# Sums of merged blocks formed behind the merges and kept in DRAM, one plain output pair in place of two, and three planner costs

## The chip, the core and the metric

The kernel runs on one core of a Trainium2 chip. The metric is the device time of one execution in microseconds; three runs of the kernel before the change took 1144.78, 1145.87 and 1147.69 us, median 1145.87.

## What is computed

One encoder layer is applied to two batches with the same weights: a prompt of 512 tokens and a sample of 1024, 1024 channels wide, all in float32.

```python
h = rmsnorm(x, norm_g)
qa, ka, va, za, qb, kb, vb, zb, ga, gb = split(h @ w_in)
oa = (neighbourhood_attention(rms(qa), rms(ka), va, rpb) * silu(za)) @ w_o_a
ob = (window_gqa_attention(rms(qb), rms(kb), vb, t5, sink) * silu(zb)) @ w_o_b
merged = sigmoid(ga) * oa + sigmoid(gb) * ob
y = x + merged @ w_out
```

The last line is the one on which most of the change bears: for the sample, merged is 1024 x 1024 and w_out is 1024 x 1024.

## The kernel before, in words

Every operand of a matmul is held as a high part (rounded to fp32r) and a low part (the rest), and a product is made of three matmuls: high x high, high x low, low x high (`product`, L1276). The step that makes the two parts is `split` (L1163): ACT copies the high part, then DVE or POOL subtracts it from the source to give the low part. In the names, `hh` and `hl` are the parts of the normed input, and later of the merged values, which take its place; `whi` and `wlo` are those of a weight; `T` holds both parts of a moving operand that was made by sums or loaded; `U`, `C`, `S`, `ot` and `raw` are tiles of 128 x 512 in pools of 4, 5, 3, 2 and 4 buffers; `p`, `x` and `d` are the 2, 5 and 1 PSUM banks.

The stages follow each other: the prompt's attention, the prompt's dense phase, the sample's attention, the sample's dense phase (`dense_phase`, L1136). In a dense phase the output projections are done in pairs of 128-channel chunks, in one of two ways. A plain pair (`pair_classic`, L1308) takes two chunks x two halves of the tokens x eight blocks of channels x three matmuls of 512 columns. A pair by Strassen's scheme (`pair_strassen`, L1320) takes seven products of four blocks x three matmuls: product 0 on the merged block (0,0), 1 on (1,0), 2, 3, 4 and 5 on the sums T1, T2, T0 and T3, and 6 on (1,1). It needs four sums of weights per pair (tiles `S`), and, once for all pairs, the four sums of merged blocks, each in four pieces k (`sums`, L1185): T0 = (0,1) - (0,0), T2 = (1,1) - (0,1), T1 = (1,1) - T0, T3 = T1 - (1,0). A piece takes 10 steps on DVE or POOL, since the high and low parts are added up one after the other, and then four splits into `T`. The eight `T` buffers hold the branch outputs until the last merge has read them.

A merge m (L1543) makes chunk m of the merged values: two products per half, gate values loaded back from `g_d` into `C` and `U`, two multiplications, one addition, one split into hh and hl. Merges run from m = 0 to 7 at priorities 12 to 19, the four output pairs at 20 to 23. `CLASSIC_S` = (1, 0, 2) says how many pairs of the sample are plain: one of the z projections, none of the gates, two of the output.

The order of all instructions on all five queues is made ahead of time by a list scheduler (`Flow`, L141): each operation has a list of engines with a cost in ns, a priority (lower first), the tiles it makes and reads, and what it must follow. When an engine is free in the planner's clock, it takes the ready operation of the lowest priority number for which buffers are free. DVE and POOL don't run steps with two SBUF operands at the same time in this plan. The attention's costs of ACT, DVE and POOL are multiplied by `SLACK` = 1.1. The plan fixes the order alone; on the chip each engine runs its own queue in order and waits for semaphores. All DMAs are issued by SP, in order. So a changed cost changes the order, here of both attention phases, and no work.

In the attention (`attention_phase`, L648) the steps named in the change are: the low parts of k and of q (DVE, L887 and L901, in `make_qk`), the strided copies `hb` of hh and hl that branch B reads (ACT L662 or DVE L664, in `project`), and the copies that turn rows into bias tables (ACT L662, in `tables`).

Of the kernel before, what the change touches and what calls it, by code (L numbers as in the profile page):

```python
# [10 lines left out]
F32 = mybir.dt.float32  # L11
# [16 lines left out]
SCRATCH = 1024  # L28
CLASSIC_P = (4, 8, 4)
SIDE = {5: 0, 8: 1, 11: 2, 15: 3}  # L30
CLASSIC_S = (1, 0, 2)
LEFT_PAD = 56
WAKE = 0
SOON = 10
# [106 lines left out]
class Flow:  # L141
# [46 lines left out]
    def dma(self, emit, nbytes, prio, **kw):  # L188
        return self.op((("sp", 470),), lambda e: emit(), prio, lag=nbytes / 360, **kw)
# [165 lines left out]
def encoder_kernel(  # L355
# [292 lines left out]
    def attention_phase(geo, hh, hl, h_ops, mask_d, early, late):  # L648
# [24 lines left out]
        def tables(br, g, prio):  # L673
            nb_t = tile_([P, max(2 * at[-1], 4 * GW)], F32, "bias", 2)
            first = [nb_t]
            for i in range(2 if br == "A" else 4):
                raw = tile_([P, max(GW, 48 * geo.cw)], F32, "raw", RAW[nt])
                if br == "A":
                    run, cw = 3 * geo.cw * 16, geo.cw
                    h = 2 * g + i  # L680
                    sp(
                        lambda raw=raw, h=h: nc.sync.dma_start(raw.t[:, :run], rpb_x[nt][h]),
                        run * 512, prio, new=[raw], after=expanded[nt, h],
                    )
                    for o, n, c0 in [(a + o, n, c0) for a, (_, runs) in zip(at, a_tables) for o, n, c0 in runs]:
                        nw = n // P * cw
                        for l in range(2):

                            def emit(e, i=i, o=o, n=n, c0=c0, nw=nw, l=l, raw=raw):
                                rv = raw.t[:, :run][:, ::-1].rearrange("p (c h l) -> p c l h", l=2, h=8)  # L690
                                rv = rv[:, c0 : c0 + nw, l, : geo.rh]
                                ov = nb_t.t[:, i * at[-1] + o : i * at[-1] + o + n]
                                ov = ov.rearrange("p (c l h) -> p c l h", l=2, h=geo.rh)[:, :, l]
                                mv = mask.t[:, o : o + n].rearrange("p (c l h) -> p c l h", l=2, h=geo.rh)[:, :, l]
                                engines[e].tensor_tensor(ov, mv, rv, op=ALU.subtract)

                            f.op(
                                (("dve", DVE_(n // 2)), ("pool", POOL_(n // 2))), emit, prio,
                                new=first, use=[raw, mask], into=[nb_t],
                            )  # L700
                            first = []
                else:
                    h = 4 * g + i

                    def emit_load(raw, h, lo):
                        ld = line_d[h : h + 1, :]
                        src = bass.AP(tensor=ld.tensor, offset=ld.offset + lo * 64, ap=[[1, 64], [1, GW]])
                        nc.sync.dma_start(raw.t[:, :GW].rearrange("(c l) f -> l c f", l=2)[lo], src)

                    for lo in range(2):  # L710
                        kw = {"new": [raw], "after": line_op} if lo == 0 else {"into": [raw]}
                        sp(lambda raw=raw, h=h, lo=lo: emit_load(raw, h, lo), 98304, prio, **kw)

                    def emit(e, i=i, raw=raw):
                        ov = nb_t.t[:, i * GW : (i + 1) * GW].rearrange("p (w c l) -> p w c l", w=3, l=2)
                        rv = raw.t[:, :GW][:, ::-1].rearrange("p (w l c) -> p w c l", w=3, l=2)
                        copy(e, ov, rv)

                    f.op((("act", ACT_(GW)),), emit, prio, new=first, use=[raw], into=[nb_t])
                    first = []  # L720
            return nb_t

# [5 lines left out]
        def project(br, w, t, prio):  # L728
# [5 lines left out]
            if br == "A":  # L734
                hs = h_ops[t]
                part = [lambda k, v=v: v.t[:, k, t * P : (t + 1) * P] for v in (hh, hl)]
                held = [[hh] * KC, [hl] * KC]
                done = {}
            else:

                hs = []
                hb = [[tile_([P, KC // 2, P], F32R, "hb", HB) for _ in range(2)] for _ in range(2)]
                part = [lambda k, v=v: v[k // 4].t[:, k % 4] for v in hb]
                held = [[v[k // 4] for k in range(KC)] for v in hb]
                done = {}
                for q in range(2):
                    for m, v in enumerate((hh, hl)):
                        done[m, q] = f.op(
                            (("act", 960), ("dve", DVE_(512))),
                            lambda e, m=m, v=v, q=q: copy(  # L750
                                e, hb[m][q].t, v.t[:, 4 * q : 4 * q + 4, t:nt:nb].bitcast(F32)
                            ),
                            prio - 1, new=[hb[m][q]], hold=[v], after=[o for u in h_ops.values() for o in u], port=True,
                        )
# [92 lines left out]
        def make_qk(br, gi, t, qk, prio):  # L847
# [23 lines left out]
            elif whole:  # L871
# [11 lines left out]
                prio, use=[pt, gains_v], after=old, **kw,  # L883
            )
            b = f.op(
                (("dve", DVE_(P) + 165),),
                lambda _: dve.scalar_tensor_tensor(  # L887
                    kt.t[:, k0 + 1, tok], pk(), gain_k[br], kt.t[:, k0, tok].bitcast(F32), op0=ALU.mult, op1=ALU.subtract
                ),
# [2 lines left out]
            for s in slots:  # L892
# [4 lines left out]
                prio, use=[pt, gains_v], into=[q],  # L897
            )
            f.op(
                (("dve", DVE_(n) + 165),),  # L900
                lambda _: dve.scalar_tensor_tensor(  # L901
                    qv(1), pts(), gain_q[br], qv(0).bitcast(F32), op0=ALU.mult, op1=ALU.subtract
                ),
# [232 lines left out]
    def dense_phase(geo, hh, hl, h_ops, o_stores, exps_done, start, opened, tp, up, p0, p1, p2, x_t, y_t, classic, fill, after_gates=None, side=None):  # L1136
# [7 lines left out]
        short = nt == nh  # L1144
        any_tt = lambda n: (("dve", DVE_(n)), ("pool", POOL_(n)))
        u_d = dpool.tile([8, P, nt], F32, tag=f"u_d{nt}", name=f"u_d{nt}")
        g_d = dpool.tile([2, 8, P, nt], F32, tag=f"g_d{nt}", name=f"g_d{nt}")
        stores = {}
        h_reads = []
# [32 lines left out]

            return mov

        def sums(prio, done):  # L1185

            tv = [tuple(f.value(tp, [P, 4, sn], F32R, "T", 8) for _ in range(2)) for _ in range(4)]
            ops = {}
            for k in range(4):
                blk = lambda a, kk, n: (lambda: a.t[:, kk, n * sn : (n + 1) * sn].bitcast(F32))  # L1190
                h = {(i, n, a): blk((hh, hl)[a], k + 4 * i, n) for i in range(2) for n in range(2) for a in range(2)}
                t = [tile_("S", 3) for _ in range(4)]

                def step(j, in0, block, part, op, new, other=None):
                    after = done[k + 4 * block[0], block[1]] if done else []
                    kw = {"new": [t[j]]} if new else {"into": [t[j]]}
                    use = [v for v in (other, None if new else t[j]) if v]
                    tt(
                        lambda v=t[j]: v.t[:, :sn], in0, h[*block, part], op, sn, prio, use=use, after=after, hold=[hh, hl], **kw
                    )  # L1200


                for j, plus, minus in ((0, (0, 1), (0, 0)), (2, (1, 1), (0, 1))):
                    after = done[k + 4 * plus[0], plus[1]] + done[k + 4 * minus[0], minus[1]] if done else []
                    tt(
                        lambda v=t[j]: v.t[:, :sn], h[*plus, 0], h[*minus, 0], ALU.subtract, sn, prio, new=[t[j]], after=after,
                        hold=[hh],
                    )
                    step(j, lambda v=t[j]: v.t[:, :sn], plus, 1, ALU.add, False)
                    step(j, lambda v=t[j]: v.t[:, :sn], minus, 1, ALU.subtract, False)  # L1210
                after = done[k + 4, 1] if done else []
                tt(
                    lambda v=t[1]: v.t[:, :sn], h[1, 1, 0], lambda v=t[0]: v.t[:, :sn], ALU.subtract, sn, prio,
                    new=[t[1]], use=[t[0]], after=after, hold=[hh],
                )
                step(1, lambda v=t[1]: v.t[:, :sn], (1, 1), 1, ALU.add, False)
                step(3, lambda v=t[1]: v.t[:, :sn], (1, 0), 0, ALU.subtract, True, t[1])
                step(3, lambda v=t[3]: v.t[:, :sn], (1, 0), 1, ALU.subtract, False)
                for j in (0, 2, 1, 3):
                    vh, vl = tv[j]  # L1220
                    ops[j, k] = split(
                        lambda vh=vh, k=k: vh.t[:, k], lambda vl=vl, k=k: vl.t[:, k], lambda v=t[j]: v.t[:, :sn], sn, prio,
                        (vh, k == 0), (vl, k == 0), [t[j]],
                    )

            return moving_sums(tv, ops)

# [352 lines left out]
                side(12 + m)  # L1580

        h_reads = []
        mov_h, mov_t = blocks(m_ops, nh), sums(20, m_ops) if o_classic < 4 else None
        for i in range(4):
            srcs = [[w_out[c, j] for j in range(2)] for c in (2 * i, 2 * i + 1)]
            post = lambda m, *a, i=i: post_out(2 * i + m, *a)
# [185 lines left out]
```

## Time and profile before

| | |
|---|---|
| median of three runs | 1145.87 us (1144.78 to 1147.69) |
| profiled execution, its own time | 1146.52 us |
| its span, first to last instruction | 1144.7 us |
| granted TensorE clock, mean | 1.000 |
| matmuls in the span | 6139 |

A record of a matmul lasts longer than the distance to the next one, since matmuls are pipelined; the distance between starts is what counts. The same holds, in a smaller measure, for steps of DVE and ACT. In lists of waits the columns are the total, the number of waits and the longest, in us.

### The profile page before, as it was taken

To read this page: it belongs to the slowest core of one execution; us is meant where nothing else is said; L and a number is where in the kernel's file an instruction comes from. 1 tells how busy PE (TensorE), PEld (TensorE's weight loads), DVE (VectorE), ACT (ScalarE), POOL (GpSimd) and SP (SyncE) were. 2 spreads that over 40 slices of the span, in tenths; PEclk is the share of its full clock that TensorE was granted. 3 is DMA by queue.
4 is the path that set the end of the run, shared out by engine and by line. 5 is a ranking of instruction groups with operands and counts; after the bars stand their busy time and mean duration, and the time that the engine had idled before them with its cause. 6 is when DMAs were issued, how large, how long until landed. Compare 5 with 4: busy or idle time off the path is not lost.

```text
span 1144.7 us, 18482 instructions
## 1 busy us (share of the span) xinstructions
PE 1133.8 (99%) x6139; PEld 985.8 (86%) x6139; DVE 854.4 (75%) x1975; ACT 644.9 (56%) x1467; POOL 308.3 (27%) x413
## 2 busy tenths in 40 slices
PE   8999999999999999999999999999999999999998
PEld 6999988888888899999999888888888888788887
DVE  5888798497765468887778888865878755497984
ACT  5777987544433346665678988865534434343320
POOL 3653433000010054343333445330222210132110
PEclk9999999999999999999999999999999999999999
DMA  7854543488786422121221213226657335573072
GB/s 253 273 158 141 181 113 102 115 264 266 232 277 199 165 72 67 25 70 32 71 61 50 56 37 93 56 66 214 218 148 211 129 111 159 200 238 121 29 223 90
DMA packets 124705, 159.86 MB, mean 140 GB/s; under 512 B 28297, under 2 KB 66961, under 8 KB 124610
## 3 DMA queue, kind: packets, MB, share of 16 engines
q1 hardware_dynamic: 124610, 158.69, 45.4%
q8 instruction: 48, 0.79, 0.3%
q14 instruction: 47, 0.39, 0.1%
HBM read 121.93 MB, written 41.44 MB: 143 GB/s over the span
## 4 chain that ended last, share of the span: by engine, by line
PE 94%; DVE 2%; DMA 2%; ACT 1%; POOL 1%; issue 0%; SPq 0%; ACTq 0%; POOLq 0%
PE p L761 25%; PE x L1285 9%; PE x L1286 9%; PE x L1284 9%; PE x L1063 5%; PE x L1026 5%; PE x L934 4%; PE p L1284 4%; PE p L1285 4%; PE d L1284 4%; PE p L1286 4%; PE d L1286 4%; PE d L1285 4%; PE x L861 2%; DMA ot<-u_d 1%; DMA w<-in_w_att_dram 1%
## 5 line engine op out<-in xcount | busy, mean ns | idle before, releaser
L761 PE MATMUL p<-whi,hh 128*128 128x384 f32 x384 | 133.4, 348 | 0.0
L761 PE MATMUL p<-wlo,hh 128*128 128x384 f32 x384 | 133.1, 347 | 0.0
L761 PE MATMUL p<-whi,hl 128*128 128x384 f32 x384 | 132.4, 345 | 0.0
L978 ACT ACTIVATE sb<-sb,mx 128x384 f32<-128x384 f32 (+1 forms) x192 | 107.5, 563 | 22.4 <-DVE mx L969 22.2
L1167 ACT ACTIVATE whi<-raw 128x512 fp32r<-128x512 f32 (+1 forms) x140 | 81.1, 590 | 52.6 <-PE x L1285 26.2
L761 PE MATMUL p<-whi,hb 128*128 128x384 f32 x384 | 107.5, 347 | 0.0
L1172 POOL TENSOR_TENSOR wlo<-raw,whi 128x512 fp32r<-128x512 f32 (+1 forms) x29 | 40.9, 1413 | 242.4 <-ACT whi L1167 130.4
L1284 PE MATMUL x<-hh,whi 128*128 128x512 f32 x264 | 102.7, 389 | 0.0
L1285 PE MATMUL x<-hl,whi 128*128 128x512 f32 x264 | 102.7, 389 | 0.0
L1286 PE MATMUL x<-hh,wlo 128*128 128x512 f32 x264 | 102.7, 389 | 0.0
L1037 DVE TENSOR_TENSOR pp<-x,pp 128x512 fp32r<-128x512 f32 (+1 forms) x136 | 82.6, 638 | 18.9 <-ACT pp L1032 17.8
L1172 DVE TENSOR_TENSOR wlo<-raw,whi 128x512 fp32r<-128x512 f32 (+1 forms) x111 | 70.1, 645 | 30.5 <-ACT whi L1167 30.2
L1285 PE MATMUL x<-T,whi 128*128 128x512 f32 x224 | 87.5, 390 | 0.3 <-DVE T L1172 0.2
L1286 PE MATMUL x<-T,wlo 128*128 128x512 f32 x224 | 87.2, 389 | 0.0
L1284 PE MATMUL x<-T,whi 128*128 128x512 f32 x224 | 87.1, 389 | 0.0
L1032 ACT ACTIVATE pp<-x 128x512 fp32r<-128x512 f32 (+1 forms) x136 | 70.9, 560 | 22.8 <-PE x L1026 21.8
L799 POOL TENSOR_TENSOR rs_r<-rs_v,mhalf 128x4 f32<-128x4 f32 (+1 forms) x72 | 81.7, 1134 | 5.7
L1063 PE MATMUL x<-pp,v 128*128 128x256 f32 (+1 forms) x368 | 77.8, 324 | 0.8 <-DVE pp L1037 0.8
L792 POOL TENSOR_SCALAR rs_v<-ss 128x4 f32<-128x4 f32 (+1 forms) x72 | 26.2, 364 | 187.3 <-DVE ss L785 184.6
L761 PEld LDWEIGHTS p<-whi,hl 128*128 128x128 f32 x384 | 73.0, 190 | 1.3 <-issue 1.0
L761 PEld LDWEIGHTS p<-wlo,hh 128*128 128x128 f32 x384 | 73.0, 190 | 1.0 <-issue 0.5
L761 PEld LDWEIGHTS p<-whi,hh 128*128 128x128 f32 x384 | 73.0, 190 | 0.9 <-issue 0.5
(351 smaller groups left out, 2985.5 us busy)
## 6 DMA issues: line engine op xcount, KB each, us to landing
raw<-in_w_g_dram SPq DMA_DIRECT2D x76, 256.0 KB
w<-in_w_att_dram SPq DMA_DIRECT2D x46, 384.0 KB
ot<-o_d SPq DMA_DIRECT2D x36, 256.0 KB
g_d<-C SPq DMA_DIRECT2D x34, 256.0 KB
raw<-in_w_z_dram SPq DMA_DIRECT2D x32, 256.0 KB
raw<-in_w_out_dram SPq DMA_DIRECT2D x32, 256.0 KB
C<-g_d SPq DMA_DIRECT2D x24, 256.0 KB
out_dram<-C SPq DMA_DIRECT2D x23, 256.0 KB
```

Source lines behind the costliest of these rows:

```text
L761: pe.matmul(ps.t[:, :GW], part[u](k), mv.t[:, c], start=k == 0 and m == 0, stop=k == KC - 1 and m == 2,)
L799: lambda e: nc.gpsimd.tensor_tensor(r.t[:, :nn], rv.t[:, :nn], mhalf[:, :nn], op=ALU.pow),
L978: act.activation(sb.t[:, :width], sb.t[:, :width], AF.Exp, bias=mx.t[:, i : i + 1], scale=-1.0, accum_out=sm.t[:, i : i + 1],)
L1026: pe.transpose(pt.t[:, u * P : (u + 1) * P], sbs[i].t[:, c * P : (c + 1) * P], ident)
L1032: lambda e, pt=pt, pp=pp, nn=nn: act.activation(pp.t[:, 0, :nn], pt.t[:, :nn], AF.Copy),
L1037: lambda e, pt=pt, pp=pp, nn=nn: dve.tensor_tensor(pp.t[:, 1, :nn], pt.t[:, :nn], pp.t[:, 0, :nn].bitcast(F32), op=ALU.subtract),
L1063: pe.matmul(out(), v.t[:, vs], mv(), start=first, stop=last)
L1167: (("act", ACT_(n)),), lambda e: act.activation(hi(), src(), AF.Copy), prio,
L1172: lambda e: engines[e].tensor_tensor(lo(), src(), hi().bitcast(F32), op=ALU.subtract), prio,
L1284: pe.matmul(out, hi.t[:, cs], mh(), start=first and k == 0, stop=False)
L1285: pe.matmul(out, hi.t[:, cs], ml(), start=False, stop=False)
L1286: pe.matmul(out, lo.t[:, cs], mh(), start=False, stop=last and k == len(ws) - 1)
```

## The change

`CLASSIC_S` becomes (1, 0, 1): of the sample's four output pairs one is plain and three go by Strassen's scheme. The sums of merged blocks for the sample get priorities of their own, 19.2 to 19.5 for the pieces 0 to 3, which is behind merge 7 and ahead of the output pairs. The pieces 0 to 2 of the four sums are stored to a DRAM tensor `to_d` as soon as they are made, and loaded back into `U` tiles for the splits, which come at priority 20 in the order T1, T2, T0, T3; the pieces 3 stay in `S`. For the prompt nothing is stored. Three costs in the planner change: low parts of k and q from 165 to 60 ns over the size's own cost, `hb` copies on ACT from 960 to 1000 ns, bias copies on ACT by 76 ns.

```diff
-CLASSIC_S = (1, 0, 2)
+CLASSIC_S = (1, 0, 1)
...
-                    f.op((("act", ACT_(GW)),), emit, prio, new=first, use=[raw], into=[nb_t])
+                    f.op((("act", ACT_(GW) + 76),), emit, prio, new=first, use=[raw], into=[nb_t])
...
-                            (("act", 960), ("dve", DVE_(512))),
+                            (("act", 1000), ("dve", DVE_(512))),
...
-                (("dve", DVE_(P) + 165),),
+                (("dve", DVE_(P) + 60),),
...
-                (("dve", DVE_(n) + 165),),
+                (("dve", DVE_(n) + 60),),
...
+        to_d = dpool.tile([4, 4, P, sn], F32, tag=f"to_d{nt}", name=f"to_d{nt}")
...
-        def sums(prio, done):
+        def sums(split_prio, done, prios=None):
...
-            ops = {}
+            ops, away, firsts = {}, [], {}
             for k in range(4):
+                prio = prios[k] if prios else split_prio
...
                 for j in (0, 2, 1, 3):
-                    vh, vl = tv[j]
-                    ops[j, k] = split(
-                        lambda vh=vh, k=k: vh.t[:, k], lambda vl=vl, k=k: vl.t[:, k], lambda v=t[j]: v.t[:, :sn], sn, prio,
-                        (vh, k == 0), (vl, k == 0), [t[j]],
+                    if prios and k < 3:
+                        away.append((j, k, dma(
+                            lambda j=j, k=k, v=t[j]: nc.sync.dma_start(to_d[j, k], v.t[:, :sn]), 512 * sn, prio, use=[t[j]]
+                        )))
+                    else:
+                        away.append((j, k, t[j]))
+            for j, k, v in sorted(away, key=lambda a: ((1, 2, 0, 3).index(a[0]), a[1])) if prios else away:
+                vh, vl = tv[j]
+                if prios and k < 3:
+                    o, v = v, tile_("U", 4)
+                    dma(
+                        lambda j=j, k=k, v=v: nc.sync.dma_start(v.t[:, :sn], to_d[j, k]), 512 * sn, split_prio, new=[v],
+                        after=[o],
                     )
+                ops[j, k] = split(
+                    lambda vh=vh, k=k: vh.t[:, k], lambda vl=vl, k=k: vl.t[:, k], lambda v=v: v.t[:, :sn], sn, split_prio,
+                    (vh, j not in firsts), (vl, j not in firsts), [v],
+                )
+                firsts[j] = True
...
-        mov_h, mov_t = blocks(m_ops, nh), sums(20, m_ops) if o_classic < 4 else None
+        mov_h, mov_t = blocks(m_ops, nh), sums(20, m_ops, [19.2 + 0.1 * k for k in range(4)]) if o_classic < 4 else None
```

The first place is DVE's queue behind the last merge's low part (`hl_...`), before the change: sums (S) and splits (T) of the pieces 2 and 3, in front of the first additions to the output.

```order
L1161 TENSOR_TENSOR S_13005<-hh_3330,S_12975 128x512
L1172 TENSOR_TENSOR T_12766<-S_12975,T_12758 128x512
L1161 TENSOR_TENSOR S_13005<-S_13005,hl_3331 128x512
L1172 TENSOR_TENSOR T_12809<-S_12981,T_12797 128x512
L1161 TENSOR_TENSOR S_13025<-S_13005,hh_3330 128x512
L1172 TENSOR_TENSOR T_12820<-S_13005,T_12811 128x512
L1161 TENSOR_TENSOR S_13025<-S_13025,hl_3331 128x512
L1161 TENSOR_TENSOR C_12680<-x_12822,C_12680 128x512
L1161 TENSOR_TENSOR C_12716<-x_12868,C_12716 128x512
```

All sums are made before the first plain product's result (x_12822) is taken from its bank. The same queue after the change, from the last pieces of T1 (T_12852, high part T_12782) and T2 (T_12952) on; T0 is T_13001 and T3 is T_13042.

```order
L1162 TENSOR_TENSOR C_12744<-x_12887,C_12744 128x512
L1173 TENSOR_TENSOR T_12852<-S_12935,T_12782 128x512
L1173 TENSOR_TENSOR T_12952<-U_12910,T_12937 128x512
L1173 TENSOR_TENSOR T_12952<-U_12913,T_12937 128x512
L1173 TENSOR_TENSOR T_12952<-S_12899,T_12937 128x512
L1173 TENSOR_TENSOR T_13001<-U_12950,T_12980 128x512
L1162 TENSOR_TENSOR C_12795<-x_12939,C_12795 128x512
```

The row that ends T1 stands 15 rows behind the last merge's low part, the row that ends T2 three rows later. Somewhat later on the same queue stand the ends of T0 and T3 and the low parts of the first weight sums, `wlo_13024` being read by product 2 of the first Strassen pair.

```order
L1173 TENSOR_TENSOR T_13001<-U_12988,T_12980 128x512
L1162 TENSOR_TENSOR S_13031<-S_13031,hl_3330 128x512
L1173 TENSOR_TENSOR T_13042<-U_12994,T_13026 128x512
L1162 TENSOR_TENSOR S_13050<-raw_12696,raw_12768 128x512
L1173 TENSOR_TENSOR T_13042<-U_13010,T_13026 128x512
L1173 TENSOR_TENSOR T_13042<-U_13022,T_13026 128x512
L1173 TENSOR_TENSOR T_13042<-S_13031,T_13026 128x512
L1162 TENSOR_TENSOR C_12842<-x_12997,C_12842 128x512
L1162 TENSOR_TENSOR S_13082<-raw_12667,raw_12696 128x512
L1162 TENSOR_TENSOR C_12880<-C_12880,U_13076 128x512
L1173 TENSOR_TENSOR wlo_13024<-S_13070,whi_12974 128x512
```

Splits of loaded pieces (from U) now stand between the additions of the plain pair, and four rows separate the end of T3 from `wlo_13024`. The third place is SP's queue during the last merge, before:

```order
L1563 DMA C_12592<-g_d1024_94 128x512
L1563 DMA U_12623<-g_d1024_94 128x512
L1563 DMA C_12642<-g_d1024_94 128x512
L1249 DMA raw_12647<-in_w_out_dram 128x512
L1563 DMA U_12666<-g_d1024_94 128x512
```

and after, where the stores of the sums (`to_d1024_95<-S`) stand between the merge's gate loads:

```order
L1225 DMA to_d1024_95<-S_12605 128x512
L1580 DMA U_12627<-g_d1024_96 128x512
L1225 DMA to_d1024_95<-S_12597 128x512
L1580 DMA C_12651<-g_d1024_96 128x512
L1225 DMA to_d1024_95<-S_12635 128x512
L1266 DMA raw_12667<-in_w_out_dram 128x512
L1580 DMA U_12683<-g_d1024_96 128x512
```

Three stores now stand in front of the last gate load, U_12683.

## The prediction

> **What bounds the kernel now.** I read the page first: the busy line, the slices of TensorE (PE) and the shares of the chain that ended last.
>
> ```profile
> PE 1133.8 (99%) x6139; PEld 985.8 (86%) x6139; DVE 854.4 (75%) x1975; ACT 644.9 (56%) x1467; POOL 308.3 (27%) x413
> PE   8999999999999999999999999999999999999998
> PE 94%; DVE 2%; DMA 2%; ACT 1%; POOL 1%; issue 0%; SPq 0%; ACTq 0%; POOLq 0%
> ```
>
> PE is busy in every slice and is 94% of the chain. A busy PE may still wait inside its records, so I then asked for PE's own waits, which is the whole list:
>
> ```profile
> PE x L1629 <- DMA rb<-in_norm_row_dram: 4.4, 1, 4.4
> PE x L861 <- DVE qk L816: 1.0, 2, 0.5
> PE x L532 <- DVE xt L520: 0.9, 1, 0.9
> PE x L1063 <- DVE pp L1037: 0.8, 2, 0.6
> PE x L1026 <- DVE sb L1010: 0.3, 1, 0.3
> PE x L1285 <- DVE T L1172: 0.2, 1, 0.2
> ```
>
> The first is the load at the start; the other five lines sum to 3.2 us, all on VectorE (DVE), 3.0 of it in the start and the attention. So the kernel is bound by the number of matmuls and their spacing, and a better order of anything else can win at most about 3 us.
>
> The third view is PE's timeline of the out projection, cut to the rows at which a stage begins (start, duration, line, tile).
>
> ```profile
> 1059.71 0.39 PE L1284 MATMUL x<-hh,whi 128*128 128x512 f32 x1
> ...
> 1103.23 0.39 PE L1284 MATMUL x<-hh,whi 128*128 128x512 f32 x1
> ...
> 1108.67 0.39 PE L1284 MATMUL x<-T,whi 128*128 128x512 f32 x1
> ...
> 1122.27 0.39 PE L1284 MATMUL x<-hh,whi 128*128 128x512 f32 x1
> ...
> 1141.35 0.28 PE L1286 MATMUL p<-hh,wlo 128*128 128x256 f32 x1
> ```
>
> 1059.71 is the first matmul behind the merges. A plain pair is 2 chunks x 2 halves x 8 blocks x 3 = 96 matmuls; two of them take 1103.23 - 1059.71 = 43.52 us, which is 0.2267 us a matmul though each record lasts 0.39. The next pair has 7 products x 4 blocks x 3 = 84 matmuls and takes 1122.27 - 1103.23 = 19.04 us: 0.2267 again. There is no gap in either.
>
> **The change part by part.** *One plain pair fewer.* A plain pair (21.76 us) becomes one of seven products (19.04): 12 matmuls x 0.2267 = **-2.72 us**, straight off the path, since PE never waits there. The tail behind the last matmul (span 1144.7 - 1141.35) keeps its shape: the last pair is the same code.
>
> [...]
>
> *The sums come due earlier.* The first product that reads a sum (T) stands at 1108.67 now; with one plain pair less it is due 21.76 us sooner, at 1086.91. What DVE does meanwhile is in the 10 us windows (PE, PEld, DVE, ACT, POOL busy; clock; DMA share; GB/s) and in DVE's and GpSimd's (POOL's) timelines.
>
> ```profile
> 1030.00:1040.00 10.00, 10.00 (x46) 8.26 (x45) 9.21 (x14) 3.40 (x6) 3.48 (x2) 1.00 0.43 142
> 1040.00:1050.00 10.00, 10.00 (x46) 8.28 (x45) 6.14 (x10) 3.22 (x6) 0.00 (x0) 1.00 0.48 156
> 1050.00:1060.00 10.00, 10.00 (x46) 8.29 (x45) 7.71 (x12) 3.77 (x7) 3.55 (x3) 1.00 0.23 62
> 1070.00:1080.00 10.00, 10.00 (x46) 8.28 (x45) 10.00 (x18) 3.79 (x7) 0.00 (x0) 1.00 0.00 2
> 1080.00:1090.00 10.00, 10.00 (x46) 8.29 (x45) 10.00 (x18) 3.00 (x5) 1.00 (x1) 1.00 0.03 12
> ```
>
> ```profile
> 1059.49 1.78 DVE L1172 TENSOR_TENSOR T<-S,T 128x512 fp32r<-128x512 f32 x1
> 1061.19 0.68 DVE L1161 TENSOR_TENSOR U<-x,U 128x512 f32<-128x512 f32 x1
> 1064.10 0.68 DVE L1172 TENSOR_TENSOR hl<-C,hh 128x512 fp32r<-128x512 f32 x1
> 1064.70 0.68 DVE L1161 TENSOR_TENSOR S<-S,hl 128x512 f32<-128x512 f32 x1
> 1081.56 2.49 DVE L1161 TENSOR_TENSOR S<-S,hl 128x512 f32<-128x512 f32 x4
> ```
>
> ```profile
> 1059.04 1.68 POOL L1161 TENSOR_TENSOR S<-hh 128x512 f32<-128x512 f32 x1 [0.63 <-DVE T L1172]
> ...
> 1089.00 1.30 POOL L1172 TENSOR_TENSOR T<-S,T 128x512 fp32r<-128x512 f32 x1 [26.58 <-ACT T L1167]
> ```
>
> DVE is full behind the merges and makes sums until POOL ends the last T at 1090.30, which would be late for 1086.91. In front of 1060 it is free for 10 x 3 - (9.21 + 6.14 + 7.71) = 6.9 us of 30. A step of 512 costs DVE 0.60 us in a row (1064.10 to 1064.70). In the new order the last merge's low part (hl) is followed by 15 DVE steps up to the last low part of T1, and by 3, 7 and 6 more up to those of T2, T0 and T3. From 1064.70: T1 at 1064.70 + 15 x 0.60 = 1073.7, T2 at 1075.5, T0 at 1079.7, T3 at 1083.3. They are due at 1086.91 and then 2.72, 5.44 and 8.16 us later (12 matmuls a product), so the sums themselves have 11.8 us or more to spare. The narrow place is the step behind them on DVE: four steps after T3 comes the low part of the weight sum for the product at 1086.91, at 1083.3 + 4 x 0.60 = 1085.7. Its first use is that product's third matmul, 1086.91 + 2 x 0.2267 = 1087.36. The third of the four steps also waits for ACT's copy of the product that ends at 1086.91 - 2.72 = 1084.19, so it can hardly start before 1085.2, and some 1 us is to spare.
>
> POOL can use that up: while it ran its step at 1059.04, DVE's own took 1.70 us to the next start (1059.49 to 1061.19) in place of 0.60, so up to 1.1 us for each POOL step that overlaps, and POOL keeps some four steps there. Bounds: 0 (POOL falls into DVE's idle time) to 4 x 1.1 - 1 = +3.4 us. I take **+0.5**, near the lower end, since the row at 1089.00 shows a POOL step that wasn't stretched, 1.30.
>
> *The way through DRAM.* Twelve blocks of 256 KB go out and come back, 6.3 MB more; SyncE (SP) waits for each store's S tile before it issues, and for the store's landing before the load. Queued behind those waits on SP are the merges' gate loads (C and U from g_d) and the next weights (raw); DVE and ACT wait for the former. The 3.1 MB of stores fall into windows that carry 62 to 156 GB/s, the loads into 1062 to 1085, where the windows from 1070 on carry 2 and 12 GB/s. What a crowded queue does is seen in the window of the second plain pair and in SP's and DVE's rows there:
>
> ```profile
> 1090.00:1100.00 10.00, 10.00 (x46) 8.29 (x45) 5.90 (x10) 1.46 (x4) 1.59 (x2) 1.00 0.97 312
> ```
>
> ```profile
> 1091.41 0.44 SPq L1249 DMA_DIRECT2D raw<-in_w_out_dram  x1
> ```
>
> ```profile
> 1097.12 0.69 DVE L1161 TENSOR_TENSOR S<-raw 128x512 f32<-128x512 f32 x1 [4.06 <-DMA raw<-in_w_out_dram]
> ```
>
> Issue to use is 5.7 us where the DMA engines are 0.97 busy. The loads go through four U buffers, so the last are used three rounds of load and split after the merges' last U is read, about 1063 (two DVE steps after 1061.19): at 5.7 us a load and 1.2 a split (two steps of 0.60) that is 1063 + 3 x 6.9 = 1083.7, against 1083.3 by DVE's own steps. Cost taken: 0, hidden behind DVE's steps and the plain pair; without that cover each us of lateness there is a us of PE, bounds 0 to +3 (all three rounds a us late).
>
> [...]
>
> *Three costs in the planner.* They change no work, only the order in the attention of both batches. Rows: the low part of k, the low part of q, and ACT's copies.
>
> ```profile
> 23.68 0.35 DVE L887 SCALAR_TENSOR_TENSOR kt<-x,gcol,kt 128x128 fp32r<-128x128 f32 x1
> 23.94 0.34 DVE L901 SCALAR_TENSOR_TENSOR qt<-x,gq,qt 128x128 fp32r<-128x128 f32 x1
> ```
>
> ```profile
> L662 ACT ACTIVATE hb<-hl 128x512 fp32r<-128x512 f32 x25 | 30.3, 1217 | 0.9 <-PE p L761 0.9
> L887 DVE SCALAR_TENSOR_TENSOR kt<-x,gcol,kt 128x128 fp32r<-128x128 f32 x72 | 24.9, 345 | 14.4 <-ACT q L896 12.9 <-ACT qt L896 1.2
> ```
>
> The planner counts 68 + 1.043 x 128 = 201.5, plus 165 before and 60 now, times 1.1: 403 and 288 ns. The next step starts 260 ns later (23.68 to 23.94), so the new count is the truer one; hb on ACT goes from 1056 to 1100 against 1217 in the row. DVE is now planned for 72 x 2 x 115 ns = 16.6 us less than it was. Truer costs should remove some of the 3.0 us of waits, but a closer plan also leaves less slack: bounds -3.0 (all go) to +3.0 (as many again). I take **-0.5**, a sixth, near the middle as nothing in the trace leans far.
>
> Sum: -2.72 + 0.5 - 0.5 = -2.7 us. The profiled execution took 1146.5 us (span 1144.7 and 1.8 around it) and would take 1143.8; the median of the three runs, 1145.87, is 0.6 below it, so I predict **1143.2 us**, 0.24% less. That is less than the 0.3% (3.4 us) which a measurement of this kernel can tell from no change.
>
> **Rivals.** *The attention gives more* (chance 0.33): the truer costs remove one to three of the 3.0 us of waits. For: all of those waits are on DVE, whose steps were over-counted. Against: they are six single waits of 0.9 us at most, in an order that is now redrawn everywhere. Time 1145.87 - 2.7 - 1 to 3 = 1140 to 1142.
>
> *DVE is late for the first weight sum* (0.12): overlapping POOL steps and late U loads use up the 1 us and PE stands 2 to 4 us ahead of its first product with T1. For: DVE at 10.00 in the windows behind the merges. Against: 6.9 us free ahead of them. Time 1145 to 1147. [...]
>
> *Slower: SP holds the gate loads* (0.08). Each store waits on SP for its sum; in the new order gate loads of the last merge stand behind three such stores. PE has eight banks, 8 x 2.72 = 21.8 us of products, as cover, so this decides only once a gate load comes over 20 us late, or if DVE's extra sums delay the merges steadily. If each of the last four merges loses 2.5 us, that is +10 - 2.7: 1153 us. The windows speak against it, with DMA shares of 0.23 to 0.48 there.
>
> *The change doesn't do what it says*: excluded, since the built program holds exactly 12 matmuls of 512 columns fewer.
>
> **How the numbers follow.** Forecast 0.47, more from the attention 0.33, late weight sum 0.12, held gate loads and the like 0.08. Faster by over 0.3% (under 1142.4) is the second case, with a little of the first beyond it: 0.34. Slower by over 0.3% (above 1149.3): 0.08. The same: 0.58. The range takes in the bounds of the attention downwards (-2.7 - 3.0 gives 1140.2) and the late weight sum upwards (1147): 1140.2 to 1147.3, which leaves out some 0.08 below and 0.1 above.
>
> **What would show it.** Right: PE's spacing stays 0.2267 us, the out projection behind the merges takes 21.76 + 3 x 19.04 us, and PE's list of waits has no L1284 to L1286 line over 0.5 us and about as much in the attention. Wrong: a PE wait on DVE wlo or T at the first product behind the plain pair, SP waiting on DVE S or POOL S with ACT or DVE idle for U<-g_d in the last merges, or waits in the attention that have changed by more than 1.5 us either way.

## The result: slower by 1.05%, with PE standing at two places

| | before | after |
|---|---|---|
| median of four runs, us | 1146.78 | 1159.18 |
| lowest to highest, us | 1144.78 to 1150.74 | 1156.72 to 1160.03 |
| profiled execution: its time, its span, us | 1146.52, 1144.7 | 1160.03, 1158.2 |
| granted TensorE clock, mean | 1.000 | 0.996 |
| matmuls | 6139 | 6127 |

The ratio is 1.0105, 95% interval 1.0075 to 1.0134: 12.4 us slower, with 12 matmuls fewer. The forecast was 1143.2.

The page of the changed kernel: the busy line, PE's slices, the shares of the chain that ended last.

```profile
PE 1136.8 (98%) x6127; PEld 985.7 (85%) x6127; DVE 869.1 (75%) x1986; ACT 642.5 (55%) x1472; POOL 315.4 (27%) x419
PE   7999999999998999999999999999999999999898
PE 86%; DMA 5%; DVE 4%; issue 1%; ACT 1%; POOL 1%; SPq 1%; POOLq 0%; ACTq 0%; DVEq 0%
```

Three slices are one lower than before: the first, the thirteenth (347 to 376 us) and the thirty-eighth (1071 to 1100 us). PE is 86% of the chain, where it was 94%. The list of PE's waits, without its last three lines, says for whom:

```profile
PE x L1646 <- DMA rb<-in_norm_row_dram: 4.5, 1, 4.5
PE p L1301 <- ACT whi L1168: 4.4, 1, 4.4
PE x L1301 <- ACT hh L1168: 2.9, 1, 2.9
PE p L1303 <- DVE wlo L1173: 1.5, 1, 1.5
PE x L532 <- DVE xt L520: 1.1, 1, 1.1
PE x L861 <- DVE qk L816: 1.0, 3, 0.4
PE x L1026 <- DVE sb L1010: 1.0, 1, 1.0
```

Three lines are new: `whi`, `hh` and `wlo`, 8.8 us. The waits of the start and the attention (`xt`, `qk`, `sb`, and a `kt` of 0.7) are 3.8 us where they were 3.0.

*The sample's output projection.* PE's timeline at the first product with T1, which was to start at 1094.64 + 0.23 = 1094.87:

```profile
1094.64 0.39 PE L1303 MATMUL p<-hh,wlo 128*128 128x512 f32 x1
1099.40 0.79 PE L1301 MATMUL p<-T,whi 128*128 128x512 f32 x1 [4.37 <-ACT whi L1168]
1099.99 0.63 PE L1302 MATMUL p<-T,whi 128*128 128x512 f32 x1
1102.13 0.79 PE L1303 MATMUL p<-T,wlo 128*128 128x512 f32 x1 [1.51 <-DVE wlo L1173]
1102.72 0.63 PE L1301 MATMUL p<-T,whi 128*128 128x512 f32 x1
1103.15 0.63 PE L1302 MATMUL p<-T,whi 128*128 128x512 f32 x1
```

PE waits 4.37 us for the high part of the first weight sum and 1.51 for its low part, and the matmuls behind it start 0.43 us apart in place of 0.23. Why ACT made that high part so late, from ACT's timeline:

```profile
1090.21 0.64 ACT L1168 ACTIVATE T<-U 128x512 fp32r<-128x512 f32 x1 [1.93 <-DMA U<-to_d]
1092.18 1.27 ACT L1168 ACTIVATE T<-U 128x512 fp32r<-128x512 f32 x2 [1.33 <-DMA U<-to_d]
1096.42 0.63 ACT L1168 ACTIVATE T<-U 128x512 fp32r<-128x512 f32 x1 [2.98 <-DMA U<-to_d]
...
1098.73 0.62 ACT L1168 ACTIVATE whi<-S 128x512 fp32r<-128x512 f32 x1
```

ACT stands for pieces of T0 and T3, whose products come 5.4 and 8.2 us behind that of T1; `whi<-S`, which PE needs first, is queued behind them. That queue isn't the whole delay, for the weight sum that `whi` copies is itself late. Its two steps, from DVE's and POOL's timelines:

```profile
1094.84 0.69 DVE L1162 TENSOR_TENSOR S<-raw 128x512 f32<-128x512 f32 x1
1095.60 1.26 POOL L1162 TENSOR_TENSOR S<-S,raw 128x512 f32<-128x512 f32 x1 [7.65 <-DVE S L1162]
```

It is there at 1095.60 + 1.26 = 1096.86, 2.0 us behind the due time, and stands on ACT's queue for 1.9 us more. DVE has the same order:

```profile
1076.12 0.69 DVE L1173 TENSOR_TENSOR hl<-C,hh 128x512 fp32r<-128x512 f32 x1
1086.65 0.69 DVE L1173 TENSOR_TENSOR T<-S,T 128x512 fp32r<-128x512 f32 x1 [0.79 <-ACT T L1168]
...
1098.98 0.69 DVE L1173 TENSOR_TENSOR T<-S,T 128x512 fp32r<-128x512 f32 x1
1101.39 1.96 DVE L1173 TENSOR_TENSOR wlo<-S,whi 128x512 fp32r<-128x512 f32 x4
```

These are the last merge's low part, the ends of T1 and of T3, and the first weight sum's low part. PE's first output matmul stands at 1067.67; counted from there the last low part of T1 starts at +19.0, that of T3 at +31.3 and `wlo` at +33.7. The forecast (from 1059.71) had their ends at +14.0, +23.6 and +26.0, so their starts 0.6 us earlier, for a product due at +27.2. So `wlo` starts 8.3 us later than forecast: 4.1 us of that are there at the last merge's low part (+8.5 in place of +4.4), the rest comes behind it.

*The prompt's output projection*, a place the prediction doesn't speak of. The row behind the longest wait, from PE's timeline:

```profile
364.38 0.79 PE L1301 MATMUL x<-hh,whi 128*128 128x512 f32 x1 [2.92 <-ACT hh L1168]
```

PE stands 2.92 us for `hh` of the last merge, which needs its gate load. SP's queue, the last gate load of the prompt before and after:

```profile
345.20 0.61 SPq L1563 DMA_DIRECT2D ot<-g_d  x1
```

```profile
355.18 0.33 SPq L1580 DMA_DIRECT2D ot<-g_d  x1
```

PE's first output matmul of the prompt stands at 351.61 before and at 355.75 after. So the load was issued 6.4 us ahead of it before, and 0.6 us ahead after; the sigmoid, two multiplications, the addition and the split into `hh` follow it.

The distances of neighbouring matmuls beyond their usual spacing, summed by stretches of 50 us, place the loss: 6.8 and 1.5 us more in the sample's output projection (1050 to 1150), 5.7 in the stretch from 350, 3.1 in the start and the first 200 us, and 3.0 less in the rest; less 2.72 of matmuls, that is 11.4 of the span's 13.5 us; the other 2 us this count doesn't place.

### The profile page after: what moved, and what is told of

Same layout as the page of the kernel before. It is cut to its first block, busy times and chain, and to the rows that moved or that the text cites. A ratio compares the mean times of both kernels' runs of the same rounds, so it can differ in the third digit from the quotient of the medians.

```text
span 1158.2 us, 18534 instructions
## 1 busy us (share of the span) xinstructions
PE 1136.8 (98%) x6127; PEld 985.7 (85%) x6127; DVE 869.1 (75%) x1986; ACT 642.5 (55%) x1472; POOL 315.4 (27%) x419
## 4 chain that ended last, share of the span: by engine, by line
PE 86%; DMA 5%; DVE 4%; issue 1%; ACT 1%; POOL 1%; SPq 1%; POOLq 0%; ACTq 0%; DVEq 0%
PE p L761 23%; PE x L1302 8%; PE x L1301 8%; PE x L1303 8%; PE x L1063 5%; PE x L1026 5%; PE x L934 4%; PE d L1301 4%; PE d L1303 4%; PE p L1303 4%; PE d L1302 4%; PE p L1302 4%; PE p L1301 4%; PE x L861 2%; DVE S L1162 1%
## 5 line engine op out<-in xcount | busy, mean ns | idle before, releaser
L1173 POOL TENSOR_TENSOR wlo<-raw,whi 128x512 fp32r<-128x512 f32 (+1 forms) x32 | 44.2, 1383 | 287.2 <-ACT whi L1168 168.2
L1301 PE MATMUL x<-hh,whi 128*128 128x512 f32 (+1 forms) x268 | 104.3, 389 | 2.9 <-ACT hh L1168 2.9
L1302 PE MATMUL x<-hl,whi 128*128 128x512 f32 (+1 forms) x268 | 104.2, 389 | 0.3 <-DVE hl L1173 0.3
L1303 PE MATMUL x<-hh,wlo 128*128 128x512 f32 (+1 forms) x268 | 103.9, 388 | 0.0
L1173 DVE TENSOR_TENSOR wlo<-raw,whi 128x512 fp32r<-128x512 f32 (+1 forms) x108 | 69.2, 651 | 33.7 <-ACT whi L1168 33.5
L1302 PE MATMUL x<-T,whi 128*128 128x512 f32 x228 | 89.0, 390 | 0.4 <-DVE T L1173 0.2
L1301 PE MATMUL x<-T,whi 128*128 128x512 f32 x228 | 88.7, 389 | 0.0
L799 POOL TENSOR_TENSOR rs_r<-rs_v,mhalf 128x4 f32<-128x4 f32 (+1 forms) x72 | 84.8, 1178 | 5.6
L792 POOL TENSOR_SCALAR rs_v<-ss 128x4 f32<-128x4 f32 (+1 forms) x72 | 20.6, 287 | 203.7 <-DVE ss L785 201.8
```

The costliest lines, as they stand in the source:

```text
L799: lambda e: nc.gpsimd.tensor_tensor(r.t[:, :nn], rv.t[:, :nn], mhalf[:, :nn], op=ALU.pow),
L1173: lambda e: engines[e].tensor_tensor(lo(), src(), hi().bitcast(F32), op=ALU.subtract), prio,
L1301: pe.matmul(out, hi.t[:, cs], mh(), start=first and k == 0, stop=False)
L1302: pe.matmul(out, hi.t[:, cs], ml(), start=False, stop=False)
L1303: pe.matmul(out, lo.t[:, cs], mh(), start=False, stop=last and k == len(ws) - 1)
```

## The experiments

All ratios are to the kernel before, on the same chip, with their 95% intervals; "us" are differences of the medians. Where the edit is against e2, e2's edit is in it.

**e1: the three costs alone**, and **e2: everything but the costs.**

```diff
 # e1, on the kernel before
-  ACT_(GW), 960, DVE_(P) + 165, DVE_(n) + 165
+  ACT_(GW) + 76, 1000, DVE_(P) + 60, DVE_(n) + 60
 # e2, on the changed kernel: the same four back
```

> The kernel before with the three planner costs alone (two plain pairs, sums as before). Theory A (two separate losses: the new costs re-draw the order in the prompt's dense phase and the attention, and the sums are late in the sample's output projection): +8 us (6 to 10), about 1154, with a stand of PE of about 3 us ahead of the prompt's output projection near 360 us, and no gap in the sample's. Theory B (the whole loss lies in the output projection and what its longer DVE queue does; the prompt's stall is one execution's chance): 0, within 1.5 us of 1146.

Measured: 1153.94 against 1145.59, +8.3 us, ratio 1.0070 (1.0049 to 1.0091). No gap in the sample's output projection; near 360 us:

```profile
360.95 0.50 PE L1284 MATMUL x<-hh,whi 128*128 128x512 f32 x1 [1.91 <-ACT hh L1167]
```

By the count of distances above, the stretch from 350 us holds 4.3 us more than before, of the 6.3 us by which the profiled span is longer. The rest this count doesn't place.

> The changed kernel with the three planner costs as before: one plain pair, sums behind the merges and through DRAM. Theory A: the output projection alone loses 8.3 us of lateness and wins 2.7 us of matmuls, +5.6 us (4 to 7), about 1152; no stand near 360 us; PE still waits for whi and wlo ahead of the first product with T1. Theory B: +11 to +13, as the change whole.

Measured: 1152.55, +7.0 us, 1.0058 (1.0035 to 1.0080). No stand near 360, and PE's waits in the output projection are those of the change:

```profile
PE p L1301 <- ACT whi L1168: 4.0, 1, 4.0
PE p L1303 <- DVE wlo L1173: 1.5, 1, 1.5
```

What follows: two losses at two places from two parts of the change; theory B falls. They sum to 15.3 against 12.4 measured, within the intervals.

**e3: the pair alone**, and **e4: the sums' new way alone.**

```diff
 # e3, on the kernel before          # e4, on e2
-CLASSIC_S = (1, 0, 2)              -CLASSIC_S = (1, 0, 1)
+CLASSIC_S = (1, 0, 1)              +CLASSIC_S = (1, 0, 2)
```

> The kernel before with one plain pair in place of two and nothing else: sums as before, not stored, at the output pairs' priority, old costs. Theory A1 (the order of splits and weight sums behind the merges makes the stand): the sums end near 1090.3 by the trace of before against 1086.9 where the first is due, so 2 to 5 us of PE's stand and slow matmuls behind it, less 2.7: between 0 and +3 us. Theory A2 (the way through DRAM makes it): the sums come in time, -2.7 us, about 1143.

> The changed kernel with two plain pairs and the old costs: the sums behind the merges and through DRAM alone, with 21.8 us more before they are due. Theory A1 (lateness against the due time): the stand is covered, 0 us (-1 to +1). Theory A2 (the stores, loads and sums themselves hold up PE, by a crowded queue or late merges, wherever they are due): +3 us or more.

Measured: e3 +7.8 us, 1.0066 (1.0043 to 1.0088), with one wait of 7.1 us for `wlo` two matmuls into the second product of that pair. e4 +0.5 us, 1.0005 (0.9993 to 1.0017), with no wait in the output projection. So the way through DRAM costs nothing where it is covered, and the old sums without it are late by as much; A1 had the sign of e3, but at most +3 us.

**f1, f6: order and loads.** On e2:

```diff
 # f1: splits of T0 and T3 behind the first Strassen pair's weight sums (20.5)
+                split_prio = sprio0 + (0.7 if prios and j in (0, 3) else 0)
 # f6: a third of the loads into the idle ot tiles
-                    o, v = v, tile_("U", 4)
+                    o, v = v, tile_("ot", n_ot) if (k + j) % 3 == 2 else tile_("U", 4)
```

> The changed kernel with the old costs (e2, +7.0 us) and the splits of T0 and T3 at priority 20.7 in place of 20, behind the first Strassen pair's weight sums at 20.5. Theory A1 (the order of the splits, which PE does not need yet, ahead of the weight sums makes the stand): most of the 5.5 us of waits and the slow matmuls behind them go, -1 to +2 us against the kernel before. Theory A2 (the loads through four U tiles come late, whatever stands behind them): ACT and DVE are still held by U, +5 to +7 us. Theory A3 (DVE and POOL slow each other while the sums are made, so all is some 5 us late before the splits begin): +4 to +7 us.

> As e2, but a third of the loads from DRAM go into the two ot tiles, which lie idle by then, so six pieces can be under way in place of four; order of priorities as in e2. Theory A2: the splits no longer wait for loads, -2.7 to 0 us against the kernel before. Theory A1: the weight sum still stands behind the splits, +4 to +7. Theory A3: +4 to +7.

Measured: f1 +3.7 us, 1.0024 (1.0010 to 1.0037); f6 +6.2 us, 1.0050 (1.0038 to 1.0061). By the medians the order of the splits is worth 3.3 of the 9.7 us that e2 lost on top of its gain, though the intervals of e2 and f1 just touch. In f1 PE still waits 3.6 us for the same high part: the weight sums need `S` tiles, and the last pieces of the sums hold them. f6's 0.8 us lie within the intervals, and its stand has moved: PE waits 6.0 us once, in that pair's product 0, for the low part of a weight. So f6 shows that six tiles don't remove the lateness, and no price of the loads.

**f4, g5, g2, g3, g4: without POOL.** On e2:

```diff
 # f4, g5: low-part additions of the sums on DVE only
-                    tt(lambda v=t[j]: v.t[:, :sn], in0, h[*block, part], op, sn, prio, ...)
+                    f.op((("dve", DVE_(sn)),), ...)
 # g2, g3, g4: no POOL from the first merge to the plain output pair
-        any_tt = lambda n: (("dve", DVE_(n)), ("pool", POOL_(n)))
+        any_tt = lambda n, prio=0: (("dve", DVE_(n)), ("pool", POOL_(n)))[: 1 if not short and 12 <= prio < 21 else 2]
 # g3 and g5: with f1 and f6; g4: with f1
```

> As e2, but the additions of the sums that have a block of hh or hl as their second part go on DVE alone; only the first subtraction of a sum may still go on POOL. Theory A3: DVE's steps stay at 0.60 us, T1 is split some 4 us sooner, and the stand shrinks to 0 to 2 us, total -1 to +2 us against the kernel before. Theory A1 or A2: DVE has more to do and the stand stays or grows, +6 to +9.

Measured: f4 +1.7 us, 1.0020 (1.0003 to 1.0036). Its low-part additions read the blocks of the last piece in all four pieces, so its time is that of the same work on other blocks; g5 has the right ones.

> e2 with the low-part additions of the sums on DVE alone (as f4, here of the right blocks), the splits of T0 and T3 late (as f1) and six tiles for the loads (as f6); POOL keeps the splits. By the orders the first weight sum's parts stand ahead of most of T3's. Theories A1 to A3 together: -2.7 to 0 us against the kernel before. If f4's waits in the merges (hl, 2.2 us) and at the first weight sum (1.3 us) stay: +1 to +2 us.

Measured: g5 +2.7 us, 1.0025 (1.0015 to 1.0035): its second clause came true, with waits for the last merges' `hl` (1.4 us) and for the first weight sum (2.3).

> As e2 (old costs), but from the first merge to the plain output pair every step that could go on DVE or POOL goes on DVE. Theory A3 (a POOL step takes more from a full DVE, about 1.1 us, than the 0.60 us that it saves): T1 is ready earlier, the stand shrinks, 0 to +4 us against the kernel before where e2 has +7. Theory A4 (DVE has simply too much work, with POOL's help or without): more work on DVE makes the sums later, +8 us or more, with waits of PE on DVE in the merges.

Measured: g2 1143.23 against 1146.71, **-3.5 us**, 0.9970 (0.9958 to 0.9983), faster than both kernels. PE's waits of g2, whole:

```profile
PE x L1646 <- DMA rb<-in_norm_row_dram: 4.7, 1, 4.7
PE x L861 <- DVE qk L816: 1.0, 2, 0.5
PE p L1303 <- DVE wlo L1173: 1.0, 1, 1.0
PE x L1063 <- DVE pp L1037: 0.8, 2, 0.6
PE x L1302 <- DVE T L1173: 0.4, 2, 0.2
PE x L1026 <- DVE sb L1010: 0.3, 1, 0.3
```

The reason stands in one row of the windows view each: the 43.5 us of the sample's merges (PE, PEld, DVE, ACT, POOL busy; clock; DMA share; GB/s) in the kernel before, in e2 and in g2.

```profile
1016.20:1059.70 43.50, 43.50 (x193) 36.03 (x192) 34.77 (x51) 16.23 (x29) 11.29 (x8) 1.00 0.51 162
```

```profile
1014.90:1058.40 43.50, 43.50 (x193) 36.03 (x192) 40.70 (x52) 14.50 (x26) 23.11 (x15) 1.00 0.69 214
```

```profile
1014.70:1058.20 43.50, 43.50 (x194) 36.03 (x193) 41.99 (x70) 15.60 (x28) 0.00 (x0) 1.00 0.67 220
```

In e2 DVE does 52 steps in 40.70 us, 0.783 us each, and POOL 15: 67 together. In g2 DVE alone does 70 in 41.99, 0.600 each. So each of POOL's 15 steps cost DVE (0.783 - 0.600) x 52 / 15 = 0.63 us, and would itself have cost DVE 0.60. By this estimate POOL's help is nothing here, and a step that went on POOL was done later: 1.5 to 1.7 us for one, by the means of e2's forms; two are in its timelines of DVE and POOL.

```profile
1047.16 1.78 DVE L1173 TENSOR_TENSOR hl<-C,hh 128x512 fp32r<-128x512 f32 x1
1048.86 0.68 DVE L1162 TENSOR_TENSOR C<-x,C 128x512 f32<-128x512 f32 x1
```

```profile
1046.72 1.67 POOL L1162 TENSOR_TENSOR S<-S,hl 128x512 f32<-128x512 f32 x1 [3.16 <-DVE S L1162]
1048.36 1.74 POOL L1173 TENSOR_TENSOR wlo<-raw,whi 128x512 fp32r<-128x512 f32 x1
```

While POOL ran the step at 1046.72, the last link of that merge (`hl`) took 1.70 us to the next start (1047.16 to 1048.86) in place of 0.60. In g2 the last `hl` stands 4.4 us behind PE's first output matmul and T1's last split 11.6 us behind it; in e2 8.0 and 18.8.

> g2 with the splits of T0 and T3 behind the first Strassen pair's weight sums (as f1) and six tiles for the loads (as f6). If A1, A2 and A3 each hold a share of the stand, the three together leave less than any alone: -2.7 to +1 us against the kernel before; if A4 holds, as g2.

> g2 with the splits of T0 and T3 at priority 20.7, behind the first Strassen pair's weight sums, and four tiles for the loads as in the change. What is left in g2 is one wait of 1.0 us for the low part of that pair's raw weights; if it goes: -3.5 to -4.5 us against the kernel before, about 1142; if the redrawn order puts another wait in its place: -2.5 to -3.5.

Measured: g3 -3.0 us, 0.9969 (0.9959 to 0.9980); g4 -1.6 us, 0.9984 (0.9973 to 0.9994). g3 has no wait at the first weight sum, but a wait of 1.0 us in the prompt's attention that g2 doesn't have: once POOL is out, order and loads bring nothing more. g4 missed its range; it too has no wait at that weight sum and one of 1.5 us in the prompt's attention.

Each of these edits also redraws the order, so one faster kernel could be luck. All kernels with one plain pair say the same: the seven in which POOL keeps steps beside the merges (after, e2, e3, f1, f4, f6, g5) have a wait of PE of 1.4 to 7.1 us in the output projection, the five without (g2, g3, g4, h2, h5) none over 1.0 us. g3 and g5 share the late splits and the six tiles; with no POOL step in the merges' 43.5 us g3 has -3.0, with 10 g5 has +2.7.

**h1: POOL out of the kernel before**, where nothing is late: the edit of g2 on the kernel before.

> The kernel before (two plain pairs, old sums, old costs) with the steps that could go on DVE or POOL put on DVE from the first merge to the plain output pairs, as in g2. Theory A3 (DVE without POOL is only needed where the sums are due early): PE had no wait there, so 0 us, within 1 us. Rival (keeping POOL out is worth its 3 us by itself, whatever the number of plain pairs): -2 us or more, and g2 owes nothing to the pair by seven products.

Measured: +0.1 us, 0.9998 (0.9984 to 1.0013), theory A3. g2's gain needs the pair by seven products; POOL alone is worth nothing.

**hb_only, qk_only, h7, i1: the costs one by one.** On the kernel before:

```diff
 # hb_only          # qk_only                  # h7                       # i1: hb and bias copies
-  960              -  + 165 (q and k)         -  + 165 (q and k)         -  960,  ACT_(GW)
+  1000             +  + 60                    +  + 75                    +  1000, ACT_(GW) + 76
```

> The kernel before with one cost changed, hb on ACT 960 to 1000 ns. Theory B1 (the loss of 8 us in e1 comes from the low parts of q and k counted too short for what the chip needs): 0, within 1.5 us. Theory B2 (the loss comes from the re-drawn order as such, which any change of a cost in the attention brings): some other time, 2 us or more away from 1145.6 in either direction, with the sample's norm loads and the merges' gate loads moved against PE near 300 to 360 us.

> The kernel before with the low parts of q and k counted at 60 in place of 165 ns over their size's own cost, nothing else. Theory B1 (this count makes the 8 us of e1: the prompt's norm and merge chains are ordered later against PE): +6 to +9 us with a stand of PE near 360 us. Theory B2 (the re-drawn order as such, each set of costs its own draw; hb alone drew -1.6): any time, and the stand near 360 us need not be there.

> The kernel before with the low parts of q and k counted at 75 ns over their size's own cost, in place of 165 (before) and 60 (qk_only, +6.2 us): 15 ns from the one that lost. Theory B1 (a count that is too short for the chip makes the loss, in proportion): +5 to +6 us. Theory B2 (each set of costs is a draw of the order): some other time, and the stand near 360 us gone or of another length.

> The kernel before with the costs of hb (1000 ns) and of the bias copies (+76 ns), without that of q and k. Theory B1 (each cost has its own price, which add up: +8.3 for three, +6.2 for q and k, -1.6 for hb, so +3.7 for the bias copies): +2.1 us. Theory B2 (each set of costs is a draw of the order): no reason for +2.1; the time goes with the place of the prompt's last gate load against PE's last merge, a stand near 360 us if the load is issued less than some 4 us ahead, none if it is more.

Measured: hb_only -1.6 us, 0.9987 (0.9975 to 0.9999); qk_only +6.2, 1.0054 (1.0038 to 1.0071); h7 +0.6, 1.0008 (0.9993 to 1.0023); i1 +2.3, 1.0024 (1.0009 to 1.0040). 15 ns on one cost (h7 against qk_only) are worth 5.6 us, so theory B1 falls for q and k. i1 has the 2.1 us that a sum of prices gives, but not for B1's reason: its profiled execution has the same stand near 360 us without the new count of q and k. Five of i1's ten executions, with a granted clock of 1.000, take 1145.7 to 1147.4 us, and five with 0.998 to 0.999, the profiled one among them, 1149.1 to 1154.1. What sets the five apart isn't shown: in the profiled one PE's starts are 0.23 us apart again at 365.60, behind the stand, and its longest wait for `xt` is 1.4 us.

What goes with the stand is the lead of the prompt's last gate load on PE's first output matmul. From SP's and PE's timelines, in us, with PE's wait for `hh`:

| kernel | load issued | PE there | lead | wait |
|---|---|---|---|---|
| h7 | 345.60 | 353.28 | 7.7 | none |
| before | 345.20 | 351.61 | 6.4 | none |
| hb_only | 345.81 | 350.37 | 4.6 | none (0.2 for `hl`) |
| qk_only | 353.04 | 355.79 | 2.8 | 2.3 |
| i1, profiled | 354.61 | 357.21 | 2.6 | 2.3 |
| e1 | 352.05 | 354.12 | 2.1 | 1.9 |
| after | 355.18 | 355.75 | 0.6 | 2.9 |

The other kernels fit: h5, with the three costs, has a lead of 1.4 us and a wait of 2.5; the twelve with the old costs or with hb alone have leads of 4.3 to 7.0 us and no wait for `hh` over 0.3. In the profiled executions the stretch from 350 us holds 5.0 of the 8.1 us that qk_only's span is longer than before, and 3.2 of i1's 7.6.

The row of SP's queue for h7, 15 ns away from qk_only, to be read beside those of before and after above:

```profile
345.60 0.33 SPq L1563 DMA_DIRECT2D ot<-g_d  x1
```

**h2, h5: the two places together.** h2 is g2 with hb at 1000; h5 is the changed kernel with POOL kept out as in g2.

> g2 with hb on ACT counted at 1000 ns, the one of the three costs that drew -1.6 us by itself. If the two places are independent: -3.5 - 1.6 = -5.1 us against the kernel before, about 1141.5. If the cost is a new draw each time: anywhere between -5 and 0.

> The changed kernel as it is, all three new costs, with POOL kept out from the first merge to the plain output pair. If the two losses are independent: -3.5 (g2) + 8.3 (e1) = +4.8 us against the kernel before, about 1151, with the stand of PE near 360 us as the only long one left. If the stand in the output projection depends on the costs too: +7 us or more.

Measured: h2 -1.9 us, 0.9979 (0.9967 to 0.9991), so hb's gain doesn't add to g2's, as the clause of a draw had it. h5 +2.5 us, 1.0020 (1.0003 to 1.0038): without the stand in the output projection the changed kernel keeps that near 360 us as its only long wait (2.5 us for `hh`), less than the +4.8 of a plain sum, though the intervals of g2 and e1 leave room for it. Beside g2, the three costs take 2.5 + 3.5 = 6 us there.

## Why the prediction was wrong, step by step

*One plain pair fewer, -2.72.* Right. g2 takes it: -3.5 us (its interval is -4.8 to -1.9) with 1.0 us of one new wait.

*The sums come due earlier, +0.5, bounds 0 to +3.4.* This step failed. The mechanism was named (POOL stretches DVE's steps, here 1.70 us for 0.60, and the first weight sum is late), and its place (`whi` and `wlo` of the first product with T1), as the rival with chance 0.12. Its size was 9.7 us (e2's +7.0 and the -2.72 that it hid), for three reasons. The count of POOL's steps: "some four" were allowed for, and 15 stand in the merges alone (8 before), since the sums now run beside them; at 0.63 us each they take 9.5 us of DVE's time, which is not yet time of PE. The point from which it was counted: T1 was counted in steps behind the last merge's low part, which was taken to keep its place, 4.4 us behind PE's first output matmul; it came at 8.5, which is 4.1 of the 8.3 us by which `wlo` was late. And the price of a stand: behind a wait of 4.4 us the matmuls ran at 0.43 us for a while, 2.4 us more of loss (6.8 + 1.5 less the waits of 4.4 and 1.5) that no term held. The 0.60 us a step was right for a DVE alone.

*The splits' order.* The prediction read that the weight sum stands four rows behind T3, and priced the four rows. It did not ask what those rows wait for on ACT: loads for T0 and T3 that come 1.3 to 3.0 us late each, ahead of a step that is due first. Nor did it ask when the weight sum itself can be made: it was there 2.0 us behind the due time. f1, which changes the order alone, gives some 3 us.

*The way through DRAM, cost 0, bounds 0 to +3.* Right where it is covered (e4 +0.5, its interval holding 0). Where it isn't, no run separates it: e3, without it, is as slow as e2, and f6's stand lies elsewhere.

*Three costs in the planner, -0.5, bounds +-3.* This step failed outright: +8.3 us by e1, outside its bounds. The view was wrong, not only the size. I looked for the effect where the costs are used, in the attention's waits, and these hardly changed. The order is one list for the whole program: the prompt's dense phase was redrawn too, and not the attention phases alone, as was said ahead of the prediction. Its chain of gate load, sigmoid, merge and `hh` came some 4 to 6 us later against PE (the leads in the table), and a lead of 6.4 us was used up. The trace of before showed that lead; a bound from it would have been a stand of some us. That "truer costs should remove waits" is refuted: 60 ns is nearer to the measured 260 ns a step than 75 or 165, and is the worst of the three.

*The rival "SP holds the gate loads"* is not what happened. In the 43.5 us of the sample's merges ACT waits 15.0 us for `U<-g_d`, where it waited 14.0 before, and PE doesn't wait there. A late gate load did matter, but in the prompt, and not behind stores of sums, which the prompt doesn't have.

What stays open: which of the redrawn steps makes the prompt's chain late, and where the rest of e1's loss lies. That the short lead makes the stand is read from the leads and waits of all kernels; no run moves the lead alone. In e1, qk_only and after the sample's norm loads, which share ACT, DVE and SP with that chain, come 3 to 9 us later too, but no experiment moved them alone.

## What to carry to other kernels

Before work is moved to an earlier due time, count the steps of the helper engine that will run beside it, and price them by what they take from the main one: in the merges of e2, with DVE busy for 40.70 of 43.50 us, a step of two SBUF operands on POOL took an estimated 0.63 us from it and saved it 0.60, so the right number of POOL steps there was none. A cost in a planner is a redraw of the whole order; look for the chains with the least lead in every later stage, and expect no proportion between the cost and the time. And where a step that is due first stands in an in-order queue behind steps that wait for loads, the loads' lateness is its own: `whi` stood 1.9 us on ACT's queue.

## What the hardware showed that was not expected

The granted clock in windows of 5 us of the changed kernel, around the stand in the output projection:

```profile
1095.00:1100.00 5.00, 0.63 (x3) 0.50 (x2) 2.84 (x5) 2.78 (x5) 1.26 (x1) 0.82 0.36 114
1100.00:1105.00 5.00, 3.49 (x9) 2.29 (x8) 5.00 (x10) 2.18 (x5) 0.00 (x0) 0.50 0.59 195
1105.00:1110.00 5.00, 5.00 (x24) 4.14 (x23) 3.30 (x6) 1.67 (x5) 3.84 (x3) 1.00 0.59 175
```

The clock is 0.50 from 1100 to 1105 us, behind the stand, and 1.00 in the next window, so this stand cost more than its waits: 2.4 us more than their 5.9, by the count of distances. In e1 the starts behind a wait of 1.91 us were 0.43 us apart too (clock 0.66 from 360 to 365), while behind g5's of 1.8 us the clock stayed at 1.00. No threshold follows from that, since behind i1's wait of 2.3 us, which ended at 364.54, the starts were 0.23 us apart again at 365.60.
